# First shift and scale in four two-tile stages, the rest of the modulation as row sums

## The chip, the cores and the metric

The kernel runs on one core of one Trainium2 chip, in float32. The metric is device time in microseconds of one execution; lower is better. Weights lie in HBM and are laid out on the host before the launch.

## The reference, cut to what matters

Two transformer blocks run one after the other on 256 tokens of width 1024. The change touches only how the first block is modulated: a vector `c` gives six vectors of 1024 numbers (shift, scale and gate, twice), and `c_ctx` gives shift and scale for 256 context tokens.

```python
silu_c = jax.nn.silu(c)
silu_cc = jax.nn.silu(c_ctx)
mod = silu_c @ w_mod[layer] + b_mod[layer]               # 1024 -> 6 x 1024
sh1, sc1, g1, sh2, sc2, g2 = [m[:, None, :] for m in jnp.split(mod, N_MOD, axis=-1)]
mc = jnp.split(silu_cc @ w_mod[layer] + b_mod[layer], N_MOD)
h = modulate(rms_norm(x, norm1_w[layer]), sh1, sc1)      # h * (1 + scale) + shift
hc = modulate(rms_norm(xc, norm1_w[layer]), mc[0], mc[1])
q, k, v, g, f = split_proj(h @ wi)                       # keys and values of hc too
...
x = x + g1 * y
h2 = modulate(rms_norm(x, norm2_w[layer]), sh2, sc2)
x = x + g2 * conv_ffn(h2, ...)
```

The second block (RWKV-7, mLSTM and a layer of retrieved experts) is not touched.

## The kernel before, in words

Activations are held transposed: a "tile" is 128 features x 256 tokens, and the 1024 features are eight tiles. A product keeps float32 accuracy by a split: ScalarE casts a weight tile to a rounded high part (line 245), VectorE subtracts to get the low part (line 246), and three matmuls are accumulated (lines 267 to 269, or 277 to 279 with tokens as the output's rows). `weights` (line 248) loads a raw weight tile of 128 x 1024 numbers, 512 KB, into one of four buffers `wf`, from SP's queue, and splits it into one of three pairs of buffers `wh`, `wl`. Every product of the first block goes through these buffers. `lin_units` (line 287) is a product cut into units: each `next` does one weight tile (two of the eight feature tiles) for all output columns.

The start of the first block is lines 425 to 550. `cs` is silu of `c` and `c_ctx` side by side (line 426). `mod_first(j)` (line 438) computes 512 columns of the modulation for both vectors as a thin product on TensorE: `cs` is the stationary side with four columns (high and low parts of two vectors), the split weights stream through (lines 446 and 447); the resulting row is copied by ScalarE (line 451), transposed back into columns by TensorE (line 454) and put together with its bias by VectorE (lines 457 to 459). j = 0 and 1 are the shift, j = 2 and 3 the scale; `scales` (line 491) makes 1 + scale, times the norm's weight. `rstd` (line 328) squares the input on ScalarE and sums over features by matmuls with ones (line 325). `norming` (line 360) makes one normed and modulated feature tile per step: a VectorE product (line 365), a ScalarE add with rounding (line 370), a VectorE low part (line 371). The string `START` orders the start by hand, a letter per step: first modulation 0 and 2, then four tiles normed ("s"), the rest of the modulation and units of the query product ("q") and of the Fourier product ("f") between, and so on; "x" loads the context, "l" the constants, "c" the context's sums of squares.

The modulation's other 4096 columns are needed only later and only for `c`. `mod_rest` (line 462) computes them on VectorE: each weight tile of 128 x 512 is multiplied by a per-partition number of `cs` and added to `macc` (lines 476 and 478), eight times for 512 columns; then TensorE sums over partitions by four matmuls of `macc` with a column of ones (line 482; each fp32 matmul is two passes). Its loads (line 432) share the four `wf` buffers. It is pulled in steps by `beside` (line 563), one step per weight tile of the products that follow, about two apart, from the value product to the output product.

The tile framework orders each engine's instructions at build time, by program order as a priority and by its own estimate of when inputs are ready; at run time each engine and each DMA queue goes strictly in that order, with semaphores between. Buffers `S(shape, name)` (class `_Slots`, line 197) are slots of 2, 4 or 8 KB per partition that are handed on: a new user waits until the old one is through. SBUF has six slots of 8 KB and twelve of 4 KB here.

## Time and profile before

| what | value |
|---|---|
| median of three runs | 1500.76 us (1499.41 to 1501.85) |
| profiled execution, own time | 1506.47 us |
| span of the profiled execution | 1504.7 us |
| TensorE busy | 1352.3 us, 90% |
| VectorE busy | 1048.2 us, 70% |
| ScalarE busy | 739.0 us, 49% |
| GpSimd busy | 301.3 us, 20% |
| DMA, mean over the span | 275 GB/s |

The span is one execution taken by the hardware profiler; its own time includes what lies around the span. PE is TensorE's matmul, PEld its weight load, DVE VectorE, ACT ScalarE, POOL GpSimd, SP SyncE, which issues most loads. "Idle before" an instruction is time in which its engine had nothing running, and the name behind the arrow is what ended it. Roughly, the first block's attention and retention take to 325 us, its feed-forward part and the second block to 842 us, and the expert layer, in which the DMA engines are 99% busy with gathers, the rest.

### The profile page before, as it was taken

The page shows a single profiled execution, that of the slowest core. Times are in us where ns is not written, and L with a number is a line of the kernel's source. Part 1 is how long each engine was busy: PE and PEld are TensorE (multiplying, and loading weights), DVE is VectorE, ACT ScalarE, POOL GpSimd, SP SyncE. Part 2 cuts the span into 40 slices and gives each one's busy share as a digit, 9 for nine tenths or more (in the row PEclk, how much of TensorE's full clock was granted, in tenths as well). Part 3 has the DMA queues.
Part 4 walks back from the last instruction along what each step waited for, and adds up shares of the span by engine and source line. Part 5 has one row for each costly group of instructions (what it writes and reads, how often), then busy time and mean ns, then how long its engine had stood idle before and what let it go on. Part 6 is the DMA issues. An engine that isn't in the chain of part 4 may idle for free.

```text
span 1504.7 us, 21103 instructions
## 1 busy us (share of the span) xinstructions
PE 1352.3 (90%) x7496; PEld 975.6 (65%) x7496; DVE 1048.2 (70%) x2095; ACT 739.0 (49%) x1566; POOL 301.3 (20%) x283
## 2 busy tenths in 40 slices
PE   6999999989999999999999789878978898778786
PEld 3788898989999988899889435323533353223222
DVE  6784876867766778656478777778676775767544
ACT  7533554455555676534465355344434353434433
POOL 0000000000000000000000345443444344434341
PEclk9999999999999999999999899999999999999999
DMA  8655575745555453312147699999999999999995
GB/s 289 226 169 181 176 249 192 245 139 183 183 185 187 147 164 118 113 57 90 52 162 251 269 422 420 422 421 421 409 422 420 421 416 420 421 421 421 421 421 237
DMA packets 76569, 413.07 MB, mean 275 GB/s; under 512 B 8641, under 2 KB 8769, under 8 KB 43313
## 3 DMA queue, kind: packets, MB, share of 16 engines
q0 software_dynamic: 38880, 276.59, 44.5%
q1 hardware_dynamic: 37440, 134.88, 27.6%
q8 instruction: 59, 0.97, 0.3%
q14 instruction: 46, 0.37, 0.1%
q10 hardware_dynamic: 144, 0.26, 0.0%
HBM read 410.66 MB, written 1.05 MB: 274 GB/s over the span
## 4 chain that ended last, share of the span: by engine, by line
PE 51%; DMA 19%; DVE 11%; issue 9%; POOL 5%; ACT 4%; POOLq 0%; SPq 0%; DVEq 0%; ACTq 0%
DMA uv<-in_uv_dram,rows 17%; PE psb L267 9%; PE psb L268 9%; PE psb L269 9%; POOL uv L1487 5%; DVE uv L1494 4%; PE acc L1500 3%; DMA wf<-in_wmod_dram 2%; PE psa L277 2%; PE psa L279 2%; PE psa L278 2%; PE acc L267 1%; PE acc L269 1%; PE acc L268 1%; PE psr L1042 1%
## 5 line engine op out<-in xcount | busy, mean ns | idle before, releaser
L1500 PE MATMUL acc<-uv,dg 128*128 128x512 f32 x1024 | 501.9, 630 | 116.8 <-ACT dg L1498 114.2
L1500 PEld LDWEIGHTS acc<-uv,dg 128*128 128x128 f32 x1024 | 188.1, 196 | 419.7 <-ACT dg L1498 251.3
L1494 DVE CUSTOM_DVE_ANT_0 uv<-uv,hn 128x1024 f32<-128x1024 f32 x256 | 310.2, 1222 | 171.7 <-DMA uv<-in_uv_dram,rows 165.7
L1487 POOL DMA_INDIRECT uv<-in_uv_dram,rows x256 | 283.1, 1106 | 395.1 <-PE acc L1500 268.7
L246 DVE TENSOR_TENSOR wl<-wf,wh 128x1024 fp32r<-128x1024 f32 x213 | 258.2, 1217 | 125.8 <-ACT wh L245 122.6
L245 ACT CAST wh<-wf 128x1024 fp32r<-128x1024 f32 x213 | 221.9, 1044 | 237.3 <-PE psb L268 137.4
L267 PE MATMUL psb<-hxh,wh 128*128 128x256 f32 x960 | 280.3, 292 | 4.7 <-ACT hxh L370 3.4
L268 PE MATMUL psb<-hxl,wh 128*128 128x256 f32 x960 | 274.9, 287 | 0.0
L269 PE MATMUL psb<-hxh,wl 128*128 128x256 f32 x960 | 274.1, 286 | 0.2 <-DVE wl L246 0.2
L1495 ACT ACTIVATE act<-act 128x1 f32<-128x1 f32 x256 | 51.8, 202 | 341.4 <-DVE act L1494 341.3
L267 PEld LDWEIGHTS psb<-hxh,wh 128*128 128x128 f32 x960 | 185.4, 193 | 11.2 <-issue 4.7
L268 PEld LDWEIGHTS psb<-hxl,wh 128*128 128x128 f32 x960 | 185.3, 193 | 3.8 <-issue 2.9
L269 PEld LDWEIGHTS psb<-hxh,wl 128*128 128x128 f32 x960 | 185.2, 193 | 1.1 <-issue 0.3
L1498 ACT ACTIVATE dg<-io,act 128x128 f32<-128x128 f32 x256 | 102.8, 402 | 8.4
L1496 ACT ACTIVATE act<-act,gate 128x1 f32<-128x1 f32 x256 | 75.3, 294 | 8.3
L980 POOL MEMSET mt<- 128x2048 f32 x2 | 3.6, 1816 | 351.9 <-PE psb L269 351.9
L478 DVE SCALAR_TENSOR_TENSOR macc<-wf,cs,macc 128x512 f32<-128x512 f32 x56 | 42.0, 750 | 23.0 <-DMA wf<-in_wmod_dram 22.2
L843 POOL DMA_DIRECT2D wq<-in_wq_dram x12 | 6.3, 529 | 258.1 <-PE pstm L992 138.7
L267 PE MATMUL acc<-fh,wh 128*128 128x256 f32 x176 | 49.5, 281 | 0.0
L268 PE MATMUL acc<-fl,wh 128*128 128x256 f32 x176 | 49.4, 281 | 0.0
L269 PE MATMUL acc<-fh,wl 128*128 128x256 f32 x176 | 49.4, 281 | 0.0
L277 PE MATMUL psa<-wh,hxh 128*128 128x512 f32 x96 | 38.7, 404 | 0.0
(468 smaller groups left out, 2076.9 us busy)
## 6 DMA issues: line engine op xcount, KB each, us to landing
wf<-in_wmod_dram SPq DMA_DIRECT2D x48, 512.0 KB, 4.3
wf<-in_wup_dram SPq DMA_DIRECT2D x44, 512.0 KB, 3.6
wf<-in_win_dram SPq DMA_DIRECT2D x28, 512.0 KB, 4.5
wf<-in_wdn_dram SPq DMA_DIRECT2D x22, 512.0 KB, 3.7
wf<-in_wbg_dram SPq DMA_DIRECT2D x16, 512.0 KB, 4.6
wf<-in_wo_dram SPq DMA_DIRECT2D x16, 512.0 KB, 4.7
wf<-in_wml_dram SPq DMA_DIRECT2D x16, 512.0 KB, 3.7
wf<-in_wg_dram SPq DMA_DIRECT2D x16, 512.0 KB, 3.7
```

Of the source, the lines that this page charges most:

```text
L245: self.nc.scalar.copy(h, src)
L246: self.nc.vector.tensor_sub(l, src, h.bitcast(F32))
L267: nc.tensor.matmul(ps, p, xh[:, k0 + k, :], start=s, stop=False, skip_group_check=True)
L268: nc.tensor.matmul(ps, p, xl[:, k0 + k, :], start=False, stop=False, skip_group_check=True)
L269: nc.tensor.matmul(ps, q, xh[:, k0 + k, :], start=False, stop=e, skip_group_check=True)
L277: nc.tensor.matmul(ps, x, wh[:, k, :n], start=s, stop=False)
L1487: nc.gpsimd.indirect_dma_start(t, None, a["uv"], bass.IndirectOffsetOnAxis(ap=self.rows[b][:, h, k:k + 1], axis=0))
L1494: nc.vector.tensor_tensor_reduce(t[:, :D], t[:, :D], hn[:, b], 1.0, 0.0, ALU.mult, ALU.add, act)
L1495: nc.scalar.activation(act, act, AF.Gelu)
L1496: nc.scalar.activation(act, act, AF.Copy, scale=self.gate[b][:, h, k:k + 1])
L1498: nc.scalar.activation(dg, ident, AF.Copy, scale=act)
L1500: nc.tensor.matmul(acc[b][c], dg, t[:, D + c * 512:D + (c + 1) * 512], start=False, stop=h == PH - 1 and k == TOPK - 1, skip_group_check=True)
```

## The change

- The modulation's first 2048 columns are stored in eight pieces of 256 columns (1024 KB each), four of the shift and four of the scale. `stage(s)` computes piece s of both: two feature tiles' shift and scale at once. The raw pieces go into four 8 KB slots `wm`, loaded ahead from SP's queue, and each next one as a slot becomes free; split halves go into 4 KB slots of `S` instead of the shared pairs.
- `START` is gone. For each of four stages: `stage(s)`, two feature tiles normed, one unit of the query product, one of the Fourier product.
- The input, the context and the constants are loaded from Pool's queue instead of SP's.
- The other 4096 columns are stored transposed (`wmt`). `cr` is silu of `c` spread over all partitions as a row of 1024 numbers, made after stage 0 by eight matmuls and two copies. `mod_rest` then takes one 128 x 1024 tile per step: one VectorE instruction multiplies by `cr` and sums along the row into one column of `mod`; the bias is added after each eighth. No TensorE work is left in it. Its loads use 4 KB slots of `S` and run two tiles ahead. The number of steps stays the same.
- The square root's table is warmed after the exponentials, not between them.

```diff
-START = "ssssmqmmmnnnnqffhssssxqlfcqfqf"
...
-        "wmod": _chunks(i["w_mod"][0]), "win": _chunks(i["w_in"][0]),
+        "wmod": _chunks(i["w_mod"][0][:, :2 * D], 256),
+        "wmt": np.ascontiguousarray(i["w_mod"][0][:, 2 * D:].T).reshape(32, P, D), "win": _chunks(i["w_in"][0]),
...
+        def load(i):
+
+            if i < 8:
+                raw[i] = t = S([P, KT, 256], "wm%d" % i)
+                nc.sync.dma_start(t, a["wmod"][i // 2 + 4 * (i % 2)])
+
+        def stage(s):
 
             ps = self.ps("psm")
-            for k0 in range(0, KT, 2):
-                wh, wl = self.weights(a["wmod"][j][:, k0:k0 + 2])
-                for k in range(2):
...
+            for i in (2 * s, 2 * s + 1):
+                cols = slice(256 * (i % 2), 256 * (i % 2) + 256)
+                for j in range(2):
+                    w = raw[i][:, 4 * j:4 * j + 4]
+                    wh, wl = (S([P, 4, 256], "w%s%d" % (x, j), F32R) for x in "hl")
+                    self.split(w, wh, wl)
+                    for k in range(4):
+
+                        n = 4 * j + k
+                        nc.tensor.matmul(ps[:4, cols], cs2[:, n], wh[:, k], start=i % 2 == 0 and n == 0, stop=False, skip_group_check=True)
+                        nc.tensor.matmul(ps[:2, cols], cs2[:, n, :2], wl[:, k], start=False, stop=n == 7, skip_group_check=True)
+                    S.free("wh%d" % j, "wl%d" % j)
+                S.free("wm%d" % i)
+                load(i + 4)
             row = self.tmp([4, 512], "mrow")
             nc.scalar.copy(row, ps[:4])
...
         def mod_rest():
 
-            accs = [S([P, 512], "macc%d" % i) for i in range(2)]
-            wf = mod_load(4, 0)
...
-                for n in range(4):
-                    nc.tensor.matmul(pt[:, n:n + 1], acc[:, n * P:(n + 1) * P], ones[:, 0:1], start=True, stop=True)
-                nc.vector.tensor_add(mod[:, 4 * j:4 * j + 4], pt[:, :4], V("bmod")[:, 4 * j:4 * j + 4])
-            S.free("macc0", "macc1")
+            w = {}
+
+            def load(n):
+                if n < 48:
+                    w[n] = S([P, D], "wr%d" % n)
+                    nc.sync.dma_start(w[n], a["wmt"][n - 16])
+            for n in range(16, 18):
+                load(n)
+            for n in range(16, 48):
+                load(n + 2)
+                nc.vector.tensor_tensor_reduce(w[n], w[n], cr, 1.0, 0.0, ALU.mult, ALU.add, mod[:, n:n + 1])
+                S.free("wr%d" % n)
+                if n % 8 == 7:
+                    js = slice(n - 7, n + 1)
+                    nc.vector.tensor_add(mod[:, js], mod[:, js], V("bmod")[:, js])
+                yield
+            S.free("cr")
             yield
 
         rest = mod_rest()
...
         self.consts()
+        nc.gpsimd.dma_start(xt, a["xt"])
+        for i in range(4):
+            load(i)
...
-        nc.scalar.activation(self.warm, f2[:, :1], AF.Sqrt)
-        pulls(first, 3)()
-        nc.sync.dma_start(xt, a["xt"])
+        nc.scalar.activation(self.warm, wctx[:, 0, 0, :1], AF.Sqrt)
         r = self.rstd(xt)
...
-        for i in START:
...
+        for s in range(4):
+            stage(s)
+            next(soon)
+            next(soon)
+            next(gq)
+            next(gf)
+            if s == 1:
+                nc.gpsimd.dma_start(xct, a["ct"])
+                self.C1 = C = self.blob(a["con1"], self.v1c[1], "con1", "blob", self.wid, nc.gpsimd)
+            if s == 0:
+
+                cr = S([P, D], "cr")
+                for i in range(2):
+                    ps = self.ps("pscr")
+                    for k in range(4):
+                        nc.tensor.matmul(ps[:, k * P:(k + 1) * P], cs[:, 4 * i + k, 0:1].to_broadcast([P, P]), ident, start=True, stop=True)
+                    nc.scalar.copy(cr[:, i * 512:(i + 1) * 512], ps)
+            if s == 2:
...
+                nc.gpsimd.memset(qz[0][64:], 0.0)
+                nc.gpsimd.memset(qz[1][:64], 0.0)
                 self.busy = True
                 rc = self.rstd(xct)
                 self.busy = False
...
+        for g in (gq, gf):
+            for _ in g:
+                pass
+        hc = tuple(S([P, KT, T], "hc" + i, F32R) for i in "hl")
         late = self.norming(xct, rc, m1[:, 1], modc[:, 0:8], *hc)
```

## Rows read from the trace of the kernel before

**Rows 1.** The page: busy time of each engine, share of the span, instructions.
```profile
PE 1352.3 (90%) x7496; PEld 975.6 (65%) x7496; DVE 1048.2 (70%) x2095; ACT 739.0 (49%) x1566; POOL 301.3 (20%) x283
```

**Rows 2.** Stretches: length, busy of PE, PEld, DVE, ACT, POOL, PEclk, DMA, GB/s.
```profile
0.00:70.60 70.60, 54.30 (x257) 35.57 (x258) 47.09 (x84) 47.42 (x74) 2.09 (x6) 0.93 0.77 266
70.60:98.00 27.40, 27.40 (x166) 24.27 (x165) 22.89 (x36) 10.74 (x16) 2.36 (x2) 1.00 0.54 173
98.00:325.00 227.00, 220.01 (x1543) 202.63 (x1542) 161.49 (x283) 102.97 (x150) 3.87 (x5) 0.98 0.61 196
20.00:30.00 10.00, 4.87 (x23) 1.87 (x21) 7.82 (x7) 6.21 (x7) 0.00 (x0) 0.85 0.89 297
```

**Rows 3.** Chain of waits, 0 to 72 us: start, us, what.
```profile
2.13 6.22 DMA wf<-in_wmod_dram
21.86 6.05 DMA wf<-in_wmod_dram
```

**Rows 4.** Timeline of TensorE, 0 to 72 us: start, us, engine, line, operation.
```profile
6.28 0.59 PE L446 MATMUL psm<-wh,cs 128*4 128x512 f32 x1 [6.28 <-ACT wh L245]
7.92 0.63 PE L446 MATMUL psm<-wh,cs 128*4 128x512 f32 x1
8.35 0.63 PE L447 MATMUL psm<-wl,cs 128*2 128x512 f32 x1
30.10 0.59 PE L446 MATMUL psm<-wh,cs 128*4 128x512 f32 x1
36.70 0.39 PE L447 MATMUL psm<-wl,cs 128*2 128x512 f32 x1
36.93 0.40 PE L446 MATMUL psm<-wh,cs 128*4 128x512 f32 x1
56.20 0.28 PE L267 MATMUL psb<-hxh,wh 128*128 128x256 f32 x1
56.32 0.28 PE L268 MATMUL psb<-hxl,wh 128*128 128x256 f32 x1
61.47 3.62 PE L325 MATMUL pss<-sq,io 128*128 128x256 f32 x16
64.73 0.47 PE L267 MATMUL psb<-hxh,wh 128*128 128x256 f32 x1
70.32 0.40 PE L279 MATMUL psa<-wh,hxl 128*128 128x512 f32 x1
```

**Rows 5.** Groups by shape, 0 to 80 us: count, busy, mean ns, idle before.
```profile
L246 DVE TENSOR_TENSOR wl<-wf,wh 128x1024 fp32r<-128x1024 f32 x27 | 32.4, 1219 | 17.0 <-ACT wh L245 17.0
L245 ACT CAST wh<-wf 128x1024 fp32r<-128x1024 f32 x28 | 28.8, 1043 | 15.4 <-PE psb L268 5.5 <-DMA wf<-in_wmod_dram 3.0 <-PE psm L447 2.9
L371 DVE SCALAR_TENSOR_TENSOR hxl<-nt,mod,hxh 128x256 fp32r<-128x256 f32 x8 | 3.5, 481 | 0.4 <-ACT hxh L370 0.4
L338 DVE RECIPROCAL rstd<-rstd 128x256 f32<-128x256 f32 x2 | 3.5, 1753 | 1.7 <-ACT rstd L337 1.7
```

**Rows 6.** DMA issues: count, KB each, median us to landing.
```profile
xt<-in_xt_dram SPq DMA_DIRECT2D x1, 1024.0 KB, 10.1
```

**Rows 7.** The page's groups: row products of the experts, column products of the rest.
```profile
L1494 DVE CUSTOM_DVE_ANT_0 uv<-uv,hn 128x1024 f32<-128x1024 f32 x256 | 310.2, 1222 | 171.7 <-DMA uv<-in_uv_dram,rows 165.7
L478 DVE SCALAR_TENSOR_TENSOR macc<-wf,cs,macc 128x512 f32<-128x512 f32 x56 | 42.0, 750 | 23.0 <-DMA wf<-in_wmod_dram 22.2
```

**Rows 8.** Timeline of TensorE around one column sum of the rest.
```profile
118.86 0.40 PE L279 MATMUL psa<-wh,hxl 128*128 128x512 f32 x1
119.10 0.95 PE L482 MATMUL pst<-io,macc 128*128 128x1 f32 x8
119.91 0.48 PE L277 MATMUL psa<-wh,hch 128*128 128x512 f32 x1
```

**Rows 9.** Waits of TensorE, 75 to 325 us: total, times, longest.
```profile
PE psz L665 <- DVE fs L660: 1.6, 1, 1.6
PE psz L665 <- ACT fs L659: 1.2, 1, 1.2
```

More of the change, by code (lines that the diff above doesn't have):

```diff
@@ L428, in block1 @@
         modc = cp.tile([P, 16], F32, name="modc")
[L430 to L433 removed]
+        m1 = cp.tile([P, 2, KT], F32, name="m1")
         cs2 = cp.tile([P, KT, 4], F32R, name="cs2")
         self.split(cs, cs2[:, :, :2], cs2[:, :, 2:])
[L438 to L449 removed]
+        raw = {}
+        def load(i):
[3 more added lines that the diff above has]
+        def stage(s):
+            ps = self.ps("psm")
+            for i in (2 * s, 2 * s + 1):
[11 more added lines that the diff above has]
+                load(i + 4)
             row = self.tmp([4, 512], "mrow")
@@ new lines, in stage @@
+            pt = pt[:, :4].rearrange("p (a n) c -> p a n c", a=2)
+            js = slice(2 * s, 2 * s + 2)
+            two = lambda x: x.rearrange("p (a n) -> p a n", a=2)[:, :, js]
+            t = self.tmp([P, 2, 2, 2], "mt")
+            nc.vector.tensor_add(t, pt[:, :, :, :2], two(V("bmod")[:, :16])[:, :, :, None].to_broadcast([P, 2, 2, 2]))
+            for i, m in enumerate((mod[:, :16], modc)):
+                nc.vector.tensor_add(two(m), t[:, :, :, i], pt[:, :, :, 2 + i])
+                nc.vector.scalar_tensor_tensor(m1[:, i, js], two(m)[:, 1], 1.0, V("n1w")[:, js], op0=ALU.add, op1=ALU.mult)
@@ L485, in mod_rest @@
             yield
         rest = mod_rest()
-        m1 = cp.tile([P, 2, KT], F32, name="m1")
-        def scales(j):
-            js = slice(4 * j, 4 * j + 4)
-            for i, m in enumerate((mod, modc)):
-                nc.vector.scalar_tensor_tensor(m1[:, i, js], m[:, 8 + 4 * j:12 + 4 * j], 1.0, V("n1w")[:, js], op0=ALU.add, op1=ALU.mult)
-        first = mod_first(0)
-        next(first)
         self.consts()
+        nc.gpsimd.dma_start(xt, a["xt"])
+        for i in range(4):
+            load(i)
@@ L543, in block1 @@
                 self.busy = False
-            elif i == "h":
-                scales(1)
-            elif i == "l":
-                self.C1 = C = self.blob(a["con1"], self.v1c[1], "con1", "blob", self.wid)
-            else:
-                next(work[i], None)
+        for g in (gq, gf):
+            for _ in g:
+                pass
+        hc = tuple(S([P, KT, T], "hc" + i, F32R) for i in "hl")
         late = self.norming(xct, rc, m1[:, 1], modc[:, 0:8], *hc)
```

50 lines of the change are left out of this document (4 added, 46 removed).

## The prediction

> **What bounds the kernel now.** I read the page's engine table first: TensorE is busy 90% of the span [rows 1], so a step pays if TensorE idles, waits or runs slowly there, or if the change takes work from it. Next the table of stretches, cut where the change cuts. In the start (0 to 70.6 us) TensorE is busy 54.3 us and idle 16.3; VectorE and ScalarE are busy 47 us each and the DMA engines 77%, so no single unit fills the start. In the key product behind it (to 98 us) TensorE has no gap at all, and from 98 to 325 us it is busy 220.0 of 227 us [rows 2]. Time won in the start therefore moves everything behind it forward, and in the rest only TensorE's own work counts. The chain of waits names the start's holes: two loads of modulation weights with over 6 us each stand on it [rows 3], and between 20 and 30 us TensorE is busy 4.9 of 10 us [rows 2]. The timeline shows the second loss, TensorE's lower level (1.2 GHz): modulation matmuls of 512 columns start 0.43 us apart at 8 us and 0.23 us apart, the 2.4 GHz level, at 36.7 us [rows 4].
>
> The start's work at the upper level is 64 modulation matmuls x 0.23 = 14.7 us, 96 query matmuls of 256 columns x 0.12 = 11.5, 48 Fourier matmuls of 512 columns x 0.23 = 11.0, and two sums of squares x (64.73 - 61.47 = 3.26) = 6.5 [rows 4]: 43.7 us, the small transposes left out. The last Fourier matmul starts at 70.32 and ends the start at 70.55 [rows 4]. So 26.9 us are lost: 16.3 idle, the other 10.6 lower level and trifles.
>
> **The change part by part.** *The four stages.* Work and bytes stay the same (128 modulation matmuls of 256 columns for 64 of 512; at 0.12 for 0.23 us that is 0.6 us more). What moves is when the first query product may start: now both halves 0 and 2 of the modulation must be through (at 30.1 us the 33rd modulation matmul starts [rows 4], and only then are four of the eight input tiles normed); after, two 1 MB tiles suffice for two input tiles. When is stage 0 through? A 1 MB load took 10.1 us from issue to landing [rows 6]; issued at about 1.3 us, the first weight tile lands near 11. The DMA engines moved 266 GB/s at a share of 0.77 [rows 2], 345 GB/s if always busy, so the second tile adds 3 us, or 6 if another 1 MB from the Pool queue goes between: 14 to 17.5, I take 15. Two splits behind it (a 1.04 us cast, then two subtractions x 1.22 [rows 5]) and its last matmuls give 19 us; the first squares, cr and half the tile's matmuls lie in the waits before. TensorE then starts later than now (11 to 12 against 6.28 us [rows 4]), which is in this sum.
>
> From 19 us on TensorE has 43.7 - 16 x 0.23 - 3.26 = 36.7 us of work left. With no loss at all the start ends at 55.7. How much is lost? From 30.1 to 70.55 us before, 40.5 us passed for 43.7 - 32 x 0.23 - 3.26 = 33.1 us of work, 22% on top. With the same 22%: 19 + 44.8 = 63.8. VectorE as a second bound: 24 splits x 1.22 + 16 norm steps x 0.48 + two reciprocals x 1.75 = 40.5 us [rows 5], of which 6.6 lie before 18.5 us; the other 33.9 with 22% end at 59.9, and the last query and Fourier units (24 x 0.12 + 12 x 0.23 = 5.6 us) at 65.5. I take 64.5: **6 us won**, bounds 0 and 14.8.
>
> What is added and moved with it: the stage's row copy on ScalarE waits for TensorE, its three kinds of small sums on VectorE for the transposes; behind them in the same queues stand the next stage's casts and subtractions, and TensorE waits for those. This is the new wait, and the 22% is its price. The loads of tiles 4 to 7 wait on SP's queue until a tile has been split; behind them there stand the query, Fourier and key weights. The first input, the context and the constants (some 1 MB each by their shapes) move to Pool's queue, where nothing holds them back, so they compete with the first weight tiles; Pool's two clears of the padded queries stand behind them and are needed only after the key product. Splits with buffers of their own no longer stop SP. *cr* (8 fp32 matmuls, two copies) goes into the wait for the first weight tile: nothing. Its price without that cover lies between a group of eight one-column passes (0.95 us [rows 8]), of which it is two, and the 3.26 us of sixteen 256-column passes [rows 4]: 1.9 to 3.3. ScalarE switches its tables twice less, since the square root's warm-up now follows the exponentials; that lies in the same wait: nothing.
>
> *The rest.* Eight groups of column sums leave TensorE (line 482). Around one, a matmul starts at 118.86 and the next real one at 119.91: 1.05 us for the usual 0.23, so 0.82 each and **6.6 us** for eight [rows 8], all in stretches in which TensorE is 97 to 100% busy. Nothing takes their place there. VectorE gets 32 row products of 1024 columns, a form that takes 1.22 us in the experts, 39 us; it loses 56 x 0.75 = 42 us [rows 7] and eight scalings. It is busy 161 of 227 us there [rows 2], so this is hidden; without that cover it would gain about 3. The loads of the rest leave the four buffers that they share with all other weights and run two ahead in slots of their own. VectorE now idles 22.2 us for them in front of its column products [rows 7]. TensorE feels that once: in the Fourier step it waits 1.6 us for VectorE and 1.2 us for ScalarE [rows 9], while VectorE's queue is held by such a load. I take **2 us** of these 2.8; bounds 0 and 2.8.
>
> Sum: 6 + 6.6 + 2 = 14.6 us. Behind 325 us nothing changes; the experts wait for their gathers and start earlier by the same amount. Against the profiled execution (span 1504.7, own time 1506.47) that gives 1491.9; the median of the runs is 5.7 us below that execution, so 1500.76 - 14.6 = **1486**.
>
> **A rule against it.** Three loads go to Pool's queue, as if they then ran beside SP's. No row before has both queues busy in the start. The Trainium skill (DMA: Bandwidth & Descriptors, Issuing engines are not separate DMA queues) says that DMAs of all issuing engines run on the same 16 DMA engines and interleave. By that rule the move wins no bandwidth and delays the first weight tiles: the first rival, and 1493 for 1486.
>
> **The rivals.** *The start is as long as now.* The loads bound it: 8 x 1.05 MB of modulation, 2 x 2.1 MB of query and Fourier weights, 3 MB on Pool's queue and 0.4 of small ones make 16 MB; at the start's mean of 266 GB/s [rows 2] that is 60 us, with 2 us for the first byte 62, and the last tile's split and units (2.3 and 5.6 us) end it at 70. For it: the share of 0.77 was reached with shallow queues too. Against it: 20 to 30 us shows 297 GB/s [rows 2], and larger loads stand further ahead. It leaves 6.6 us and perhaps 1: 1493.
>
> *The start loses almost nothing.* Stage after stage keeps TensorE fed, since split buffers for several stages exist. Then 14.8 + 6.6 + 2.8 = 24.2: 1476.5. Against it: VectorE alone, with no gap, ends it at 58.
>
> *Slower: TensorE stays at the lower level.* Its place is stages 1 to 3: thin matmuls in pieces of eight, each behind a cast and a subtraction, with a wait between. Run at 0.43 instead of 0.23 us [rows 4], the 36.7 us of work take twice as long and the start ends at 92, 21.9 us later than now; less 8.6 from the rest that is 13 us slower: 1514. It decides against the change when the start passes 70.55 + 8.6 + 3 = 82 us, that is when some 26 of the 36.7 us run slowly. For it: the first 14 us of thin matmuls ran so. Against it: the same thin matmuls ran at the upper level at 36.7 us, and here query and Fourier products fill in. [...] The rows show both levels for the same instructions.
>
> **How the numbers follow.** Forecast 0.50, start as long as now 0.22, start without loss 0.15, slower 0.13. The likeliest gives 1486. Eight in ten must reach the full case below (1476.5) and the bare case above (1493) with its unknowns (the 2 us not had, cr uncovered 3.3): 1476 to 1498; the slow case is left out. A measurement of this kernel can tell about 0.2%, 3 us. Faster by more than that: the first three, less a little for a start some us longer, 0.84; within 0.05; slower 0.11.
>
> **What would show it.** The last Fourier product should start near 64 us, the first query product near 22, and the granted clock in 20 to 60 us should not fall below what it was. The first weight tile should land near 11 us; if it lands past 15, the Pool queue is the reason. No column sums between 98 and 325 us, no wait of TensorE in the Fourier step, row products near 1.22 us, and no idle time of VectorE before them. The forecast is wrong if the start ends after 70 us, and its cause is then told by TensorE's spacings (0.43) or by the loads' landings.

## The result, and the profile after

The changed kernel is slower: 1510.07 us median (1509.61 to 1514.76, five runs) against 1501.85 us for the kernel before in the same series, a ratio on record of 1.0068 with a 95% interval of 1.0048 to 1.0087 (the two medians alone give 1.0055). The forecast was 1486 us, within 1476 to 1498; the measured time lies above that range, and above the kernel before.

The profiled execution of the changed kernel has a span of 1507.2 us and an own time of 1510.0. The one shown of the kernel before is some 4 us above its median, so a second profile of the same kernel (b_again, own time 1500.6) serves for comparing stages. Against [rows 1], TensorE's busy time fell by 17 us, and yet the kernel got longer. The page of the changed kernel, its engine line and the group of the row products (columns as in [rows 7]):

```profile
PE 1335.2 (89%) x7512; PEld 971.2 (64%) x7512; DVE 1041.7 (69%) x2095; ACT 734.2 (49%) x1564; POOL 307.8 (20%) x286
...
L484 DVE CUSTOM_DVE_ANT_0 wr<-wr,cr 128x1024 f32<-128x1024 f32 x32 | 39.7, 1275 | 9.1 <-DMA wr<-in_wmt_dram 9.0
```

Three stretches follow, cut at the first rotation of a query (line 408 in both kernels, the matmul of `rope`, right behind the start), at the last rotation of a key, and at the first convolution of the feed-forward part. The changed kernel's come first (columns as in [rows 2]), with 20 to 30 us to compare with the same slice in [rows 2]:

```profile
0.00:78.60 78.60, 53.52 (x336) 42.58 (x337) 51.85 (x98) 47.25 (x78) 3.89 (x9) 0.96 0.77 292
78.60:105.80 27.20, 27.20 (x166) 24.08 (x164) 27.18 (x43) 8.54 (x11) 3.89 (x2) 1.00 0.74 259
105.80:335.30 229.50, 221.43 (x1534) 203.41 (x1533) 149.57 (x266) 103.82 (x152) 3.52 (x5) 0.98 0.51 169
...
20.00:30.00 10.00, 6.88 (x58) 5.17 (x59) 8.52 (x14) 8.75 (x12) 0.00 (x0) 1.00 0.99 392
```

The kernel before, second profile, same cuts:

```profile
0.00:69.20 69.20, 52.36 (x256) 33.73 (x257) 47.10 (x83) 47.04 (x74) 2.10 (x6) 0.95 0.79 271
69.20:96.40 27.20, 27.20 (x166) 24.06 (x164) 22.79 (x36) 10.56 (x16) 2.36 (x2) 1.00 0.53 174
96.40:328.40 232.00, 226.21 (x1598) 208.74 (x1597) 165.69 (x288) 106.66 (x155) 3.87 (x5) 0.99 0.61 195
```

So the start is 9.4 us longer (78.6 for 69.2), not 6 shorter. TensorE idles 25.1 us in it instead of 16.8 (length less busy). The key product takes the same time, and the third stretch is 2.5 us shorter where 8.6 were forecast. TensorE's work there did fall: 226.2 - 221.4 = 4.8 us; but it idles 8.1 instead of 5.8 us.

Where the start loses: VectorE and then TensorE at its end, timelines of the changed kernel (start, duration, engine, line, operation, and in brackets the idle time before it and what ended it).

```profile
65.13 0.17 DVE L467 TENSOR_TENSOR mt<-pst,vec 128x8 f32<-128x8 f32 x1 [2.15 <-PE pst L462]
67.22 1.23 DVE L484 CUSTOM_DVE_ANT_0 wr<-wr,cr 128x1024 f32<-128x1024 f32 x1 [1.92 <-DMA wr<-in_wmt_dram]
68.36 0.16 DVE L469 TENSOR_TENSOR mod<-mt,pst 128x4 f32<-128x4 f32 x1
68.70 1.22 DVE L484 CUSTOM_DVE_ANT_0 wr<-wr,cr 128x1024 f32<-128x1024 f32 x1
69.85 0.88 DVE L365 SCALAR_TENSOR_TENSOR nt<-xt,m,rstd 128x256 f32<-128x256 f32 x2
```

```profile
64.69 0.40 PE L462 MATMUL pst<-io,mrow 4*128 4x4 f32 x4 [0.66 <-ACT mrow L459]
70.92 0.80 PE L267 MATMUL psb<-hxh,wh 128*128 128x256 f32 x2 [5.83 <-ACT hxh L370]
73.01 0.41 PE L267 MATMUL psb<-hxh,wh 128*128 128x256 f32 x1
73.22 0.41 PE L268 MATMUL psb<-hxl,wh 128*128 128x256 f32 x1
```

Two row products of the rest (line 484) stand in VectorE's queue, one among the small sums of the last stage (467 and 469), one ahead of its normed tiles (365). The first waits 1.92 us for a row tile, and everything behind it waits too. TensorE then stands still for 5.83 us, and behind the wait its matmuls start 0.21 us apart, the 1.2 GHz level, until 75.1 us.

In the third stretch, VectorE and TensorE of the changed kernel around 194 us:

```profile
185.91 1.22 DVE L246 TENSOR_TENSOR wl<-wf,wh 128x1024 fp32r<-128x1024 f32 x1
193.64 1.23 DVE L484 CUSTOM_DVE_ANT_0 wr<-wr,cr 128x1024 f32<-128x1024 f32 x1 [6.50 <-DMA wr<-in_wmt_dram]
196.49 1.20 DVE L246 TENSOR_TENSOR wl<-wf,wh 128x1024 fp32r<-128x1024 f32 x1
```

```profile
194.63 0.39 PE L277 MATMUL psa<-wh,hxh 128*128 128x512 f32 x1
197.74 0.50 PE L278 MATMUL psa<-wl,hxh 128*128 128x512 f32 x1 [2.72 <-DVE wl L246]
199.21 0.63 PE L279 MATMUL psa<-wh,hxl 128*128 128x512 f32 x1
199.63 0.63 PE L277 MATMUL psa<-wh,hxh 128*128 128x512 f32 x1
```

The same happens again: a row product waits 6.50 us for its tile, a weight tile's split (246) stands behind it, TensorE waits 2.72 us for that split and then runs at the lower level (0.43 us for 512 columns) to 201 us. Of the 32 row products, 25 had run by 128 us.

### The profile page after: what moved, and what is told of

The parts are those of the page before. It is cut to its first block, busy times and chain, and to the rows that moved or that the text cites. A ratio compares the mean times of both kernels' runs of the same rounds, so it can differ in the third digit from the quotient of the medians.

```text
span 1507.2 us, 21077 instructions
## 1 busy us (share of the span) xinstructions
PE 1335.2 (89%) x7512; PEld 971.2 (64%) x7512; DVE 1041.7 (69%) x2095; ACT 734.2 (49%) x1564; POOL 307.8 (20%) x286
## 4 chain that ended last, share of the span: by engine, by line
PE 44%; DMA 23%; issue 12%; DVE 11%; POOL 5%; ACT 4%; POOLq 0%; SPq 0%; DVEq 0%; ACTq 0%
DMA uv<-in_uv_dram,rows 20%; PE psb L267 8%; PE psb L269 8%; PE psb L268 8%; POOL uv L1490 5%; DVE uv L1497 4%; PE psa L278 2%; PE psa L277 2%; PE psa L279 2%; PE acc L267 1%; PE acc L268 1%; PE acc L269 1%; DMA wr<-in_wmt_dram 1%; DMA wm<-in_wmod_dram 1%; PE psr L1045 1%
## 5 line engine op out<-in xcount | busy, mean ns | idle before, releaser
L1503 PE MATMUL acc<-uv,dg 128*128 128x512 f32 x1024 | 492.3, 619 | 126.7 <-ACT dg L1501 124.6
L1503 PEld LDWEIGHTS acc<-uv,dg 128*128 128x128 f32 x1024 | 184.0, 193 | 424.0 <-ACT dg L1501 264.7
L1490 POOL DMA_INDIRECT uv<-in_uv_dram,rows x256 | 286.7, 1120 | 390.6 <-PE acc L1503 266.8
L246 DVE TENSOR_TENSOR wl<-wf,wh 128x1024 fp32r<-128x1024 f32 x197 | 239.4, 1218 | 146.4 <-ACT wh L245 145.0
L245 ACT CAST wh<-wf 128x1024 fp32r<-128x1024 f32 x197 | 205.6, 1044 | 226.6 <-PE psb L268 135.9
L484 DVE CUSTOM_DVE_ANT_0 wr<-wr,cr 128x1024 f32<-128x1024 f32 x32 | 39.7, 1275 | 9.1 <-DMA wr<-in_wmt_dram 9.0
L278 PE MATMUL psa<-wl,hxh 128*128 128x512 f32 x96 | 38.8, 405 | 2.7 <-DVE wl L246 2.7
```

The costliest lines, as they stand in the source:

```text
L245: self.nc.scalar.copy(h, src)
L246: self.nc.vector.tensor_sub(l, src, h.bitcast(F32))
L278: nc.tensor.matmul(ps, x, wl[:, k, :n], start=False, stop=False)
L1490: nc.gpsimd.indirect_dma_start(t, None, a["uv"], bass.IndirectOffsetOnAxis(ap=self.rows[b][:, h, k:k + 1], axis=0))
L1503: nc.tensor.matmul(acc[b][c], dg, t[:, D + c * 512:D + (c + 1) * 512], start=False, stop=h == PH - 1 and k == TOPK - 1, skip_group_check=True)
```

## The experiments

The table has the marks of all kernels, each from one profiled execution, in us: end of the start (first rotation of a query), last rotation of a key, the convolution. Medians are of five to twelve executions (b_again is one); the ratio is to the kernel before in the same series.

| kernel | start ends | keys end | convolution | third stretch | median | ratio, 95% |
|---|---|---|---|---|---|---|
| before, first profile | 70.5 | 97.7 | 331.5 | 233.8 | 1501.85 | 1 |
| b_again | 69.2 | 96.4 | 328.4 | 232.0 | (1500.6) | 1 |
| after | 78.6 | 105.8 | 335.3 | 229.5 | 1510.07 | 1.0068 [1.0048, 1.0087] |
| e1_rest_behind_stage3 | 78.7 | 106.2 | 337.6 | 231.4 | 1510.26 | 1.0056 [1.0042, 1.0070] |
| e2_context_late | 74.1 | 101.6 | 331.6 | 230.0 | 1506.30 | 1.0027 [1.0014, 1.0041] |
| e3_start_only | 72.1 | 99.2 | 334.6 | 235.4 | 1509.59 | 1.0054 [1.0039, 1.0069] |
| e4_rest_only | 69.8 | 97.0 | 326.6 | 229.6 | 1503.10 | 1.0000 [0.9987, 1.0013] |
| e5_rest_paced | 75.2 | 102.5 | 326.5 | 224.0 | 1499.93 | 0.9991 [0.9981, 1.0000] |
| e6_paced_late | 71.8 | 99.1 | 323.9 | 224.8 | 1496.76 | 0.9964 [0.9951, 0.9978] |
| e7_rest_only_paced | 70.9 | 98.1 | 322.8 | 224.7 | 1498.16 | 0.9967 [0.9953, 0.9981] |
| e8_input_behind_tile1 | 73.4 | 100.7 | 324.4 | 223.7 | 1495.39 | 0.9944 [0.9929, 0.9959] |
| e9_row_first | 70.4 | 97.6 | 321.1 | 223.5 | 1495.50 | 0.9958 [0.9945, 0.9971] |
| e10_row_first_pool_input | 78.4 | 105.6 | 329.7 | 224.1 | 1502.98 | 1.0008 [0.9995, 1.0021] |
| e11_rest_in_shared_buffers | 78.0 | 105.1 | 338.7 | 233.6 | 1509.50 | 1.0044 [1.0028, 1.0061] |
| e12_context_sums_last | 66.1 | 93.4 | 317.4 | 224.0 | 1491.02 | 0.9924 [0.9910, 0.9938] |
| e13_units_one_stage_later | 65.4 (62.6) | 92.5 | 315.9 | 223.4 | 1491.13 | 0.9925 [0.9910, 0.9940] |

In e13 the rotation begins before the last Fourier products: it starts at 62.6, and 65.4 is the keys' end less 27.1 us; in the other kernels 27.1 to 27.5 us lie between the two marks.

From the convolution to the end all sixteen profiles lie between 1170.4 and 1173.9 us, without an order by kernel: behind the third stretch nothing changed that these profiles can tell. One profile is one execution, so a mark can be off by some us against the medians: the two of the kernel before end their start 1.3 us apart, and e8 and e9, which differ in the place of `cr` alone, 3.0 us at the same median.

**Theory at the outset:** the row products, freed from the four buffers that all weights share, got ahead of the last stage's work in VectorE's queue, and the stall is theirs. **Rivals:** the loads on Pool's queue lengthen the start; the four stages are longer in themselves.

*e1.* The row products may not be placed before the last small sum of the last stage.

```diff
-                nc.vector.tensor_tensor_reduce(w[n], w[n], cr, 1.0, 0.0, ALU.mult, ALU.add, mod[:, n:n + 1])
+                with self.tc.issue_after(self.sums.ins):
+                    nc.vector.tensor_tensor_reduce(w[n], w[n], cr, 1.0, 0.0, ALU.mult, ALU.add, mod[:, n:n + 1])
```

> Edit: the changed kernel, with every row product of the rest kept behind the last small sum of stage 3 in VectorE's queue. Theory A (queue): in the changed kernel a row product stands in VectorE's queue between the parts of stage 3's sums and waits for its load (landed 67.22 us), and a second one follows at 68.70; without the two the sums run at 65.3 instead of 68.4 and the input tiles 4.2 us sooner, TensorE's gap of 5.8 us before the last units shrinks to about 1.7, and the lower level behind it (0.41 for 256 columns to 75.1 us) mostly goes. Start ends at 72 to 74.5 instead of 78.6; time 1504 to 1506. Theory B (loads): the late first tiles set the start, the gap is only where the delay shows; the time stays within 1 us of 1510.

Measured 1510.26, no better. The edit was too weak to test the theory: the first product moved four instructions back, and one product still stands ahead of the normed tiles, as VectorE's timeline of this kernel shows (485 is the product):

```profile
69.33 1.22 DVE L485 CUSTOM_DVE_ANT_0 wr<-wr,cr 128x1024 f32<-128x1024 f32 x1 [1.60 <-DMA wr<-in_wmt_dram]
70.48 0.88 DVE L365 SCALAR_TENSOR_TENSOR nt<-xt,m,rstd 128x256 f32<-128x256 f32 x2
```

*e2.* The context and the constants are loaded from SP's queue, not from Pool's. The expectation says behind tile 5; by SP's timeline they went out behind all eight modulation tiles.

```diff
-                nc.gpsimd.dma_start(xct, a["ct"])
-                self.C1 = C = self.blob(a["con1"], self.v1c[1], "con1", "blob", self.wid, nc.gpsimd)
+                with self.tc.issue_after(self.tile5.ins):
+                    nc.sync.dma_start(xct, a["ct"])
+                    self.C1 = C = self.blob(a["con1"], self.v1c[1], "con1", "blob", self.wid)
```

> Edit: the changed kernel, with the context and the constants issued on SP's queue behind weight tile 5 instead of on Pool's queue at 2 us. Theory B: 2 MB less stand beside the first weight tiles; at 0.4 MB per us stage 0's sums (25.6 us) come 5 us sooner, and the start ends 5 us sooner; time about 1505. Theory A: stage 0 comes sooner too, but the last units wait for whatever stands in VectorE's queue ahead of stage 3's sums; the start gains 2 us or less; time 1508 to 1510.

Measured 1506.30, 3.8 us less. Stage 0 was hardly sooner (its transposes start at 24.6 for 25.2 us, though the input landed 1.0 us later in this execution). What moved most was the end: TensorE's last wait for a normed tile fell from 5.83 to 2.92 us.

*e3 and e4.* The two halves of the change alone: e3 has the four stages and the old column products of the rest (no `cr`), e4 the old start and the row sums (`cr` made ahead of `START`).

> Edit: the four stages, with the rest computed as before the change (column products in the four shared weight buffers, sums over partitions on TensorE; no cr). Theory A: no product of the rest can slip ahead of stage 3, so the start ends at 72 to 74, 2 to 3 us later than before the change; the rest costs what it did; time 1503 to 1505. Theory B: the start ends at 77 or later; time 1508 to 1512.

> Edit: the start as before the change, the rest as row sums with loads two ahead. The forecast's step for the rest: 6.6 us of column sums and 2 us of waits less, time 1493. Theory A, extended: row products run as far ahead as their loads allow and stand in VectorE's queue ahead of splits and small sums that TensorE waits for; some of the 8.6 us is given back, time 1496 to 1500. If the new rest costs nothing and wins nothing, 1502.

Measured 1509.59 and 1503.10. Neither half gains. Without the row products, their loads and `cr` the start ends at 72.1 us: 6.5 of the 9.4 us are gone, but it is still 2.9 longer than before. The time of e3 is 8 us above the kernel before; by its profile the start gives 2.9 of them and the third stretch 3.4, of which 2.2 are TensorE's waits for VectorE (1.38 us at 104 us and 0.8 in the Fourier step, neither in b_again). Why VectorE is late there stays open, as does the rest. In e4 the start is as before, and the gain in the third stretch is 2.4 us: a stall like that at 194 us is there without the new start too: TensorE waits 2.89 us for a split at 189 us.

*b_again.* The kernel before once more.

> The kernel before, unchanged, profiled once more. Its first profiled execution took 1506.5 us, while the runs lie between 1499 and 1506 with a median of 1502. If the 4 us lie in the start, this profile shows the last Fourier product well before 70.3 us when its own time is near 1502; if they lie in the rest of the first block or in the experts, the start ends near 70 again.

Its profile has an own time of 1500.6 us: the first profile's start was 1.3 us longer, its third stretch 1.8.

*e5 and e7.* Each row product is placed behind the split of the weight tile that it goes beside, in e5 in the changed kernel, in e7 in e4.

```diff
-        self.nc.vector.tensor_sub(l, src, h.bitcast(F32))
+        self.last = self.nc.vector.tensor_sub(l, src, h.bitcast(F32))
...
-                nc.vector.tensor_tensor_reduce(w[n], w[n], cr, 1.0, 0.0, ALU.mult, ALU.add, mod[:, n:n + 1])
+                with self.tc.issue_after(self.last.ins):
+                    nc.vector.tensor_tensor_reduce(w[n], w[n], cr, 1.0, 0.0, ALU.mult, ALU.add, mod[:, n:n + 1])
```

> Edit: the changed kernel, with each row product of the rest behind VectorE's subtraction of the weight tile beside which it is asked for, so no product stands ahead of stage 3's sums or of its normed tiles, and none runs ahead of its place. Theory A (queue): the start ends at 72 to 73 as with the start alone, and the rest gives its 6.6 us of column sums; time 1502 to 1504. Rival (the start itself): the stages cost 7 us in the median with either rest, so the order of the row products hardly matters; time 1507 to 1510.

> Edit: the start as before the change, the rest as row sums, each kept behind the subtraction of the weight tile beside which it is asked for. If products that run ahead give back what the column sums won (e4_rest_only measured no difference), this gives the 6.6 us or most of it: 1495 to 1498. If it is again 1502 to 1503, the column sums' time on TensorE was covered by another wait, or is lost to one.

Measured 1499.93 and 1498.16: 10.1 us less than the changed kernel, 4.9 less than e4. Against theory A, e5's start ends later (75.2) and its time is lower. Three views of e5: the row products' group among VectorE's up to 340 us, the third stretch, and TensorE at the end of the start:

```profile
L485 DVE CUSTOM_DVE_ANT_0 wr<-wr,cr 128x1024 f32<-128x1024 f32 x32 | 38.8, 1216 | 0.0
```

```profile
102.50:326.50 224.00, 218.85 (x1533) 201.56 (x1532) 162.25 (x288) 106.26 (x154) 3.52 (x5) 0.98 0.60 193
```

```profile
65.87 0.41 PE L462 MATMUL pst<-io,mrow 4*128 4x4 f32 x4 [0.67 <-ACT mrow L459]
67.98 0.50 PE L267 MATMUL psb<-hxh,wh 128*128 128x256 f32 x2 [1.71 <-ACT hxh L370]
```

The same 32 products of the same length now wait for nothing, TensorE's last wait is 1.71 us, and the third stretch is 8.0 us shorter than before. The edit writes out the products' places and nothing else (their slots, and so their loads, follow from these): this cause is shown, and it is worth 10 us.

*e6.* e5 and e2 together.

> Edit: both e5_rest_paced and e2_context_late. Theory A: start ends at 70 to 71, time 1499 to 1502. Rival: the 4 us of e2 alone, time 1504 to 1506.

Measured 1496.76, 3.2 us less than e5: having these loads early on Pool's queue cost that much with the products paced too. The kernel is now faster than both the kernel before and the changed one. Its start (71.8) is still 2.6 us longer than before, with both known causes gone. The next four runs ask why.

*e8.* e6 with the first input on SP's queue behind two weight tiles, so that the first casts stand ahead of the input's squares in ScalarE's queue.

```diff
-        nc.gpsimd.dma_start(xt, a["xt"])
         for i in range(4):
+            if i == 2:
+                nc.sync.dma_start(xt, a["xt"])
             load(i)
```

> As e6_paced_late (row products paced, context and constants behind weight tile 5), and the first input is issued on SP's queue behind the first two weight tiles instead of on Pool's queue ahead of them; the first four casts of stage 0 then stand ahead of the squares in ScalarE's queue. Theory A: the four stages give no gain because stage 0 begins late, behind the input and its squares (first modulation matmul 17.1 us and last 22.7 us in e6_paced_late). Then the first modulation matmul starts near 9 to 11 us, the start ends 3 to 5 us sooner (67 to 69 instead of 71.8 us), and the time is 1492 to 1494 us. Theory B: the start is bound by the sum of its loads, or by VectorE's queue from stage 1 on, whatever its order. Then stage 0's matmuls come sooner but the normed tiles wait for the input, the start still ends at 71 to 73 us, and the time stays at 1496 to 1498 us.

The first modulation matmul came 7.3 us sooner than in e6 (17.1) and stage 0's transposes 1.8 sooner (21.84 for 23.68), but the start ended at 73.4 us; the time, 1495.39, can't be told from that of e6. TensorE of this kernel, at the beginning and the end of the start, and two of its slices:

```profile
9.82 0.38 PE L453 MATMUL psm<-wh,cs 128*4 128x256 f32 x1 [9.82 <-ACT wh L245]
...
64.02 0.41 PE L462 MATMUL pst<-io,mrow 4*128 4x4 f32 x4 [0.67 <-ACT mrow L459]
66.13 0.51 PE L267 MATMUL psb<-hxh,wh 128*128 128x256 f32 x2 [1.71 <-ACT hxh L370]
```

```profile
40.00:50.00 10.00, 8.19 (x46) 7.05 (x45) 6.76 (x13) 7.07 (x12) 0.00 (x0) 0.83 0.48 161
60.00:70.00 10.00, 7.63 (x55) 6.33 (x53) 7.00 (x18) 3.83 (x8) 0.00 (x0) 0.87 0.91 308
```

What was won at the front was lost again behind it: between 40 and 50 us and at the end TensorE has gaps and the lower level. Theory A of this run wanted the end to come sooner too, and it did not.

*e9 and e10.* `cr` is made ahead of stage 0 instead of behind it, in e9 in e8, in e10 in e6.

> As e8_input_behind_tile1, and cr (eight fp32 matmuls, two copies) is made ahead of stage 0 instead of behind it, so that its matmuls fall into TensorE's wait for the first weight tile. Theory A: cr is one of the start's uncovered costs (2.05 us of TensorE behind stage 0 in e6_paced_late, with ScalarE's two copies of 0.59 us among the casts of stage 1). Then its matmuls run at 4 to 8 us, the start ends about 2 us sooner than in e8_input_behind_tile1 (71 to 72 for 73.4 us), and the time is 1493 to 1494 us. Theory B: TensorE waits for VectorE and ScalarE in the stages anyhow, so that cr lay in such a wait; then the start's end and the time stay (72.5 to 74 us, 1495 to 1496 us).

> The same move of cr, made to e6_paced_late (first input from Pool's queue, its squares ahead of the first casts). Theory A: the start ends about 2 us sooner than in e6_paced_late (69.5 to 70.5 for 71.8 us), the time is 1494.5 to 1495.5 us. Theory B: cr's copies, which now stand ahead of the first weight tile's cast in ScalarE's queue, delay the first modulation matmul by 0.6 to 1.2 us and eat part of it: 71 to 72 us, 1496 to 1497 us.

Measured 1495.50 and 1502.98. In e9 the matmuls of `cr` did fall into the wait for the first weight tile, and the time is that of e8; the profiled execution ended its start at 70.4 us, 3.0 sooner than that of e8, but the medians, of different series, show no gain; at some 2 us for each interval they could not tell one of 2 us. In e10 both expectations missed: 6.2 us slower than e6. With `cr` moved the framework also moved loads. SP's timeline of e10 and of e6 (start and time until the last of the group is issued):

```profile
3.95 1.49 SPq L257 DMA_DIRECT2D wf<-in_win_dram  x2
```

```profile
22.39 0.90 SPq L257 DMA_DIRECT2D wf<-in_win_dram  x2
```

Two query weight tiles are issued at 3.95 instead of 22.39 us, beside the first modulation tiles; the transposes of stage 0 come 2.5 us later (26.2 for 23.7) and those of the last stage 5.3 us later (67.9 for 62.6). Whether these loads are the whole reason wasn't tried.

*e11.* The changed kernel with the row tiles in the four shared buffers, one ahead, and no order written out.

```diff
-                    w[n] = S([P, D], "wr%d" % n)
+                    w[n] = self.wp.tile([P, 1024], F32, tag="wf", name="wf", bufs=4)
...
-                load(n + 2)
+                load(n + 1)
```

> The changed kernel with one thing undone: the row tiles of the rest are loaded into the four buffers that all weight tiles share, one ahead, as the rest's tiles were before, instead of into slots of their own, two ahead. The row products and everything else stay, with no order written out for them. Theory A: the loss of the changed kernel came from these slots: freed from the shared buffers, the products were placed ahead of the last stage's sums and in a run ahead of the splits. Then no product stands before the last stage's normed tiles (TensorE's last wait for a normed tile 1.7 instead of 5.8 us), VectorE does not wait for a row tile by several us, and the time is that of the paced version, 1499 to 1502 us. Theory B: the row products' number and length on VectorE, or the loads in SP's queue, make the loss whatever buffer they use; then the time stays near 1508 to 1511 us. A third way: sharing the buffers makes the weight loads of the products wait for slots; then VectorE or ScalarE wait for weight tiles (over 3 us in all, 100 to 325 us), and the time is in between.

Measured 1509.50. The places came out as the first theory said (no product before the last normed tiles, TensorE's wait there 1.7 us), the time did not. VectorE's products now wait again and again for their tile, with the splits behind them. Waits in 60 to 336 us of this kernel (483 is the product; us in total, times, longest):

```profile
DVE wf L483 <- DMA wf<-in_wmt_dram: 51.6, 28, 3.9
```

So the buffers themselves are neither the loss nor its cure. What counts is that a product stands where its tile has landed and nothing urgent is behind it, which e5 arranges. Why the start of e11 is as long as that of the changed kernel without a product in it stays open; its last transposes come at 67.4 us, as late as in e10.

*e12 and e13.* In every version with the four stages so far the last stage's modulation came last, behind the third unit and the context's sums of squares, so that nothing was left to cover the wait for its normed tiles. e12 is e8 with the context's sums asked for behind the last stage; e13 also asks for each query and Fourier unit one stage later.

```diff
             next(soon)
             next(soon)
+            if s == 3:
+                self.busy = True
+                rc = self.rstd(xct)
+                self.busy = False
...
             if s == 2:
...
-                self.busy = True
-                rc = self.rstd(xct)
-                self.busy = False
```

And in e13 alone:

```diff
-            next(gq)
-            next(gf)
+            if s:
+                next(gq)
+                next(gf)
```

> As e8_input_behind_tile1, and the context's sums of squares (16 matmul passes, 3.3 us of TensorE) are asked for behind the last stage instead of ahead of it, so that the last stage's modulation comes before them and before the third query unit. Theory A: the order of the stages makes the loss: the last stage's modulation stood behind work that could have covered the wait for its normed tiles (0.7 + 1.7 us of waits and some 1.6 us at the lower level behind them). Then TensorE's waits behind the last stage go, the start ends 3 to 4 us sooner than in e8_input_behind_tile1 (69 to 70.5 for 73.4 us), and the time is 1491 to 1493 us. Theory B: the start is bound by its loads or by VectorE; then the same waits come at another place, the start ends at 72 to 74 us and the time stays at 1494.5 to 1497 us.

> As e12_context_sums_last, and each query and Fourier unit is asked for one stage later (the first behind stage 1), so that the modulation of a stage runs ahead of the units and the last one is through while two units are left. Theory A: TensorE then always has a unit while a stage's small sums and normed tiles are made; the last stage's transposes come before 55 us, the start ends at 66 to 69 us and the time is 1488 to 1491 us. Theory B: the modulation's splits and loads come no faster than TensorE used them before, so TensorE waits for them in stages 1 and 2 (over 4 us more than in e8_input_behind_tile1 between 20 and 45 us), and the start ends at 71 us or later: 1493 to 1497 us.

Measured 1491.02 and 1491.13, 0.9924 and 0.9925: 11 us faster than the kernel before, 19 faster than the change. In e12 the start ends at 66.1 us, 7.3 sooner than in the profile of e8; the median is 4.4 us lower, and all six times of e12 lie below all six of e8. (That profile of e8 took 1.9 us more than its median, and 0.9 of the 7.3 us are there at the first matmul.) The order of the last stage against the rest of the start was the third cause, worth 3 us (by the ratios to the kernel before) to 4.4; the edit was tried on e8, not on the changed kernel alone. TensorE at the end of e12's start, and its stretch:

```profile
51.43 0.41 PE L462 MATMUL pst<-io,mrow 4*128 4x4 f32 x4 [0.20 <-ACT mrow L459]
...
57.01 3.62 PE L325 MATMUL pss<-sq,io 128*128 128x256 f32 x16
60.27 0.47 PE L267 MATMUL psb<-hxh,wh 128*128 128x256 f32 x1
```

```profile
0.00:66.10 66.10, 52.65 (x337) 41.73 (x338) 46.15 (x86) 45.04 (x74) 2.10 (x6) 0.97 0.81 304
```

The last transposes come at 51.43 instead of 64.02 us, and behind them units and the context's sums (57.01) fill the time until the normed tiles are there. After 51.43 TensorE has no wait left in the start; it idles 13.5 us in all, 9.0 of them before its first instruction. That is how the kernel before was ordered too: in b_again the last modulation transposes (line 454 there) came at 45.96 us, and TensorE ran from 46.55 us to the end of the start without a gap.

```profile
45.96 0.41 PE L454 MATMUL pst<-io,mrow 4*128 4x4 f32 x4
46.55 0.39 PE L269 MATMUL psb<-hxh,wl 128*128 128x256 f32 x1 [0.18 <-DVE wl L246]
```

That e13 shifts the units as well adds nothing that the time shows.

## Why the prediction was wrong, point by point

Of the 14.1 us by which the start missed its forecast (78.6 for 64.5), 6.2 were there when stage 0 was through and 7.9 came behind it.

*Stage 0 through at 19 us: wrong.* Its transposes start at 25.2 us. I had taken the loads for the term, and the order of the queues made it longer. The first input did land near 11 us, but its squares and a table load then stood ahead of the first casts in ScalarE's queue; the norm's reciprocal stood ahead of the second tile's splits in VectorE's; and two casts of the next stage, which waited for their weight tile, stood ahead of the stage's row copy (459), for which TensorE waited 2.27 us. ScalarE and VectorE of the changed kernel, and the row copy in e6, which waits for nothing but TensorE:

```profile
10.49 1.03 ACT L317 ACTIVATE sq<-xt 128x256 f32<-128x256 f32 x3 [5.32 <-DMA xt<-in_xt_dram]
11.96 1.28 ACT L515 ACT_TABLE_LOAD   x1
14.59 2.93 ACT L245 CAST wh<-wm 128x1024 fp32r<-128x1024 f32 x3
20.35 2.00 ACT L245 CAST wh<-wm 128x1024 fp32r<-128x1024 f32 x2 [1.52 <-DMA wm<-in_wmod_dram]
22.67 1.99 ACT L245 CAST wh<-wm 128x1024 fp32r<-128x1024 f32 x2 [0.32 <-DMA wm<-in_wmod_dram]
24.57 0.57 ACT L459 COPY mrow<-psm 4x512 f32<-4x512 f32 x1
```

```profile
17.93 1.75 DVE L338 RECIPROCAL rstd<-rstd 128x256 f32<-128x256 f32 x1
```

```profile
23.05 0.57 ACT L459 COPY mrow<-psm 4x512 f32<-4x512 f32 x1 [0.33 <-PE psm L454]
```

The first query product came at 31.5, not 22 us; before it was 33.5. e8 began stage 0 7.3 us sooner than e6 (9.8 for 17.1) and its start ended no sooner, but its stage 0 was through only 1.8 us sooner; so no run shows what a stage 0 through at 19 us would have been worth.

*22% on the start's work: off by little, and with the last stage left out.* From stage 0's transposes to the start's end the changed kernel takes 53.4 us for 36.7 of work and 2.05 of `cr`, 38% on top. With the row products paced it is 48.8 us in e5 (26.4 to 75.2) and 48.1 in e6 (23.7 to 71.8), 26 and 24%: most of the excess belongs to the next step. In e12 it is 44.9 us (21.2 to 66.1), 16%. The surcharge was taken from the old order, in which the modulation was through at 46 us and the units that follow covered each wait. I never asked what stands behind the last stage in the new order: the context's sums and the third unit ahead of it, one dependent unit behind it. The new wait was named in the prediction (row copy, small sums, normed tiles) and priced inside the 22%; at the last stage it had no cover.

*Row products "hidden": the step that failed, and that cost most.* I compared VectorE's busy time with the stretch and left out its order. The queue is strictly in order, so a product whose tile is late holds the small sums or a split behind it, and TensorE with them. e5 prices it at 10.1 us by the medians. The two profiles differ by 9.5 us: 3.4 lie in the start (TensorE's wait at its end is 4.1 us shorter, 1.71 for 5.83, but the last transposes come 1.2 us later) and 5.5 in the third stretch, of which 2.7 are the wait at 194 us and some 1.6 the lower level behind it (8 matmuls, 0.2 us more each). The other 1.2 there I have not placed, and the last 0.6 is no more than two profiles of one kernel differ.

*Column sums, 6.6 us: right.* In the third stretch TensorE's busy time falls from 226.2 to 218.9 us in e5, 7.4 us, and the 64 passes of the column sums are gone. *The wait in the Fourier step, 2 us:* mis-sized. VectorE's 1.6 us of [rows 9] are gone, but the second profile of the kernel before doesn't have them either. Of the four profiles in which the rest's loads share the four buffers three have this wait (1.6 us, 0.8 in e3, 0.7 in e11), of the twelve others none: it was real, and worth 0 to 1.6 us. ScalarE's 1.2 us stay in all. Together the third stretch gave 8.0 us for the 8.6 forecast, as soon as the products were paced; that the two agree so well is partly luck, since one term was larger and the other, against b_again, gave nothing.

*`cr` at nothing:* wrong in the reason. It ran behind stage 0, uncovered (16 passes from 25.5 to 27.6 us, 2.05 us, within the 1.9 to 3.3 given for that case); moving it into the wait (e9) moved no time that the medians can tell, so what it costs stays open below some 2 us.

*The loads on Pool's queue:* they cost 3.2 us (e5 to e6) to 3.8 (e2), and the first rival had this mechanism. The Trainium skill (DMA: Bandwidth & Descriptors, Issuing engines are not separate DMA queues) says that DMAs of all issuing engines run on the same 16 DMA engines and interleave; the trace agrees as far as it goes: with loads on both queues these engines were 99% busy from 20 to 30 us, and the casts of stage 1 waited for their tiles at 20.35 and 22.67 us. Counted from the first squares, which begin with the input's landing (10.96, 12.00, 12.11 and 11.01 us in the changed kernel, e2, e5 and e6), stage 0's transposes come 1.6 us sooner in both e2 and e6, because the casts ahead of the row copy no longer wait. The rest shows behind stage 0; in e2 TensorE's last wait in the start was 2.9 us shorter. Both edits move the loads to SP's queue and to a later time at once, and the two were not tried apart.

*The slower rival, TensorE at 1.2 GHz:* the time came out near its 1514 by luck, and by another mechanism. The granted clock was 1.00 from 20 to 60 us, and the stages' thin matmuls start 0.11 to 0.12 us apart, the 2.4 GHz level; the lower level came only behind waits. (Its sum also doubled the work where its own spacings, 0.43 for 0.23 us, make 1.87 times: 88 instead of 92 us, and 1509 instead of 1514.) The Trainium skill (TensorE: Matmul & The Clock Gate, Loop structure matters more than you think) has a loop with a long DMA wait ahead of every matmul run cold; the waits in the changed kernel's stages, 0.2 to 2.3 us and between groups of matmuls, are not that loop, and the trace shows the upper level behind them. It is not so in every version: in e8 thin matmuls of stage 2, behind a wait of 1.53 us at 29.55, ran at the lower level until 33 us.

```profile
30.28 0.41 PE L453 MATMUL psm<-wh,cs 128*4 128x256 f32 x1
30.49 0.42 PE L454 MATMUL psm<-wl,cs 128*2 128x256 f32 x1
```

The sum, as the runs have it: 8.0 us won in the third stretch once paced; 10.1 lost by the products' places; in the start, paced, 6.0 lost (75.2 for 69.2), of them 3.4 to the loads on Pool's queue (71.8 in e6). The other 2.6 go in e12, with 3.1 on top, by e8's input and the last stage's place together; of these 5.7 us the place alone is worth 3 to 4.4 by the times. 10.1 + 6.0 - 8.0 = 8.1 us slower, where 8.2 were measured; since it joins medians to marks of single profiles, so close a fit is partly luck.

## What to carry to other kernels

When work is moved onto an engine that has time to spare, read its queue and not its busy share: which instruction will stand behind each moved one, and has its input landed by then. A buffer that the moved work shared also paced it, and if it gets buffers of its own its place has to be written out. And when a chain is cut into stages, price the last stage as well as the first: ask what is left on the busiest engine to cover the last stage's waits.

## What the runs showed of the hardware

A row product took 2.05 instead of 1.22 us beside a copy on GpSimd (VectorE and GpSimd of the changed kernel):

```profile
85.46 2.05 DVE L484 CUSTOM_DVE_ANT_0 wr<-wr,cr 128x1024 f32<-128x1024 f32 x1
87.44 2.05 DVE L484 CUSTOM_DVE_ANT_0 wr<-wr,cr 128x1024 f32<-128x1024 f32 x1
```

```profile
84.47 3.95 POOL L587 COPY qz<-qt 64x1024 f32<-64x1024 f32 x2 [50.01 <-DVE qt L413]
```

The Trainium skill (SBUF — State Buffer, SBUF: two separate sides) says that a VectorE instruction with two SBUF inputs and a GpSimd instruction that reads SBUF lock a shared port pair for a whole instruction, so that one waits for the other. That fits, on both sides: two products were longer by 0.83 us each, with the products before and behind them at 1.22, and the two copies took 1.93 and 1.96 us, where in e5, with no row product beside them, they took 1.13 and 1.23:

```profile
L588 POOL COPY qz<-qt x2: 1127/1176/1225, 81.1 to 82.4; 64x1024 f32<-64x1024 f32 x2
```

TensorE had no gap there, so it cost nothing.

The DMA engines moved more than the 345 GB/s that I worked out from the start's mean: 392 GB/s in the changed kernel from 20 to 30 us, at a share of 0.99. TensorE's lower level came behind short waits too: in e8 behind one of 1.71 us, where its matmuls of 256 columns start 0.21 us apart from 67.8 to 70.8 us; in e12, without that wait, the granted clock is 1.00 there.
